# Attention in a two-layer RWKV-7/MLA decoder: the products with V of one query block written as one chain on TensorE, the later head first

## The chip, the cores and the metric

The kernel runs on one core of a Trainium2 chip. The metric is the device time of one launch in microseconds (us), lower is better. The kernel before was timed three times: median 1591.6 us, from 1591.0 to 1593.85 us.

## The reference, cut to what matters

Two decoder layers on 512 tokens of width 1024, batch 1, then a final RMSNorm. A layer is a mixer and a gated feed-forward part. The mixer has two branches: an RWKV-7 recurrence of 8 heads of 64, and MLA attention of 8 heads. Attention is causal and done in blocks of 128 queries:

```python
s = (jnp.einsum('bqhd,bkhd->bhqk', qn, k_nope)
     + jnp.einsum('bqhr,bkr->bhqk', qr, k_pe)).astype(jnp.float32) * scale
s = jnp.where(key_pos[None, :] <= q_pos[:, None], s, NEG_INF)
p = jax.nn.softmax(s, axis=-1).astype(v.dtype)
return jnp.einsum('bhqk,bkhd->bqhd', p, v)
...
merged = jax.nn.sigmoid(gate_a) * y_a + jax.nn.sigmoid(gate_b) * y_b
return merged @ w_out
```

The change concerns the last product of attention, P times V.

## The kernel before, in words

Everything is kept transposed: features on the 128 partitions, the 512 tokens along the free axis. Weights stream from memory in units of 128x1024 (`raw`); ScalarE and VectorE split each unit into a rounded part `whi` and a remainder `wlo`, activations are split likewise, and a weight block costs three matmuls in the one-pass type (lines 246 to 248, tile `acc`). These make up most of the kernel.

Attention stands in `mixer`, in `heads(p)` (line 907), called for p = 0 to 3. One call handles a pair of heads, hh = 0 and 1. It makes K and q of both heads and then goes through four query blocks b = 0 to 3, with b+1 key blocks each. For every (b, hh):

- the scores `sc` (line 929, one fp32 product of 128 x 128(b+1)),
- mask, scale and row minimum on VectorE (line 932), the exponential with its row sum on ScalarE (935), the reciprocal on VectorE (936), the scaling of P on ScalarE (937),
- the b+1 transposes of P on TensorE (line 940) into the one buffer `pt`, and a copy of `pt` into `PT` (line 942), by VectorE for b = 0 and 2, by ScalarE for b = 1 and 3. `PT` has three buffers.

Then come the 2(b+1) products with V (line 947): for every key block kb, first hh = 0, then hh = 1. The stationary side is 64 columns wide, so head 0 uses the left half of the array's columns and writes partitions 0 to 63 of `po`, head 1 the right half and partitions 64 to 127. `po` has one buffer, which is split into `oops` after the fourth block.

Around it stand the recurrence (lines 777 to 815) and its outputs: `chunk_out` (products of lines 833 and 841 into `xy`, copied by ScalarE, line 844), the group norm (lines 848 to 863, VectorE, ScalarE and a scaling on GpSimd), and `transposed` (line 869, transposes of `Z` into `xy`). Behind it are the output projections, lines 957 to 986.

The order in which the instructions stand on each engine is not the written one. A scheduler places them when the program is built: it takes instructions of different stages in turn, so that the first head pair's attention stands among the steps of the recurrence, and matmuls of lines 246 to 248 stand between attention's steps. Once placed, each engine works through its own list in that order, and an instruction waits for semaphores of other engines. Within `with tc.manual_schedule(engines={PE.engine})` TensorE's instructions keep the written order. In the kernel before, `heads` has no such block.

In the placed order of before, TensorE's list holds the products of line 947 of one block in pieces: the first product of head 0 by itself, then other work, then the rest.

Of the kernel before, what the change touches and what calls it, by code (L numbers as in the profile page):

```python
# [158 lines left out]
def build(ctx, tc, x, pos, wst, vecd, constd, out):  # L159
    nc = tc.nc  # L160
    V, A, G, PE = nc.vector, nc.scalar, nc.gpsimd, nc.tensor
# [83 lines left out]
    def mm3(ps, w, xx, first, last):  # L245
        PE.matmul(ps, w[0], xx[0], start=first, stop=False)  # L246
        PE.matmul(ps, w[0], xx[1], start=False, stop=False)  # L247
        PE.matmul(ps, w[1], xx[0], start=False, stop=last)  # L248
# [22 lines left out]
    def acc():  # L271
        return accp[-1].tile([128, 512], F32, name="acc", tag="acc")

    def split(pool, src, scale, tag, bufs=None):

        hi = pool.tile([128, 512], F32R, name="hi", tag=tag, bufs=bufs)
        lo = pool.tile([128, 512], F32R, name="lo", tag=tag, bufs=bufs)
        if scale is None:
            A.copy(hi, src)
            V.tensor_tensor(lo, src, hi.bitcast(F32), ALU.subtract)  # L280
        else:
            A.activation(hi, src, AF.Copy, scale=scale)  # L282
            V.scalar_tensor_tensor(lo, src, scale, hi.bitcast(F32), ALU.mult, ALU.subtract)
        return hi, lo
# [140 lines left out]
    def mixer(l, ops, nrm, wks):  # L425
        with ExitStack() as mx:
# [211 lines left out]
            def sc(name="sc"):  # L638
                return pb.tile([128, 512], F32, name=name, tag="sc", bufs=2)
# [7 lines left out]
            with pool(name=f"ti{l}", bufs=2) as ti, tc.manual_schedule(engines={PE.engine}):  # L647
# [94 lines left out]
                for b in range(2):  # L742
                    ps = sc()
                    for u in range(16 * b, 16 * b + 16):
                        for r0, c0 in half:
                            PE.matmul(ps[r0 + 32:r0 + 64, 32 * (u % 16):32 * (u % 16) + 32],
                                      AMu[r0:r0 + 32, u, c0 + 32:c0 + 64], T11[r0:r0 + 32, u, :],
                                      start=True, stop=True, tile_position=(r0, r0 + 32))
# [28 lines left out]
                for c in range(8):  # L777
# [22 lines left out]
                    if c < 7:  # L800
                        for p in range(4):
                            for hh in range(2):
                                hd = 2 * p + hh
# [13 lines left out]
            with pool(name=f"tb{l}", bufs=2) as tb:  # L817
                def MT(name, tag, bufs=3):
                    return tb.tile([128, 512], F32, name=name, tag=tag, bufs=bufs)
# [79 lines left out]
                Vt = tb.tile([128, 4, 512], F32, name="Vt", bufs=1)  # L899
# [7 lines left out]
                def heads(p):  # L907
                    psk = acc()
                    mm3(psk, [w[:, 128 * p:128 * p + 128] for w in lk], kvop, True, True)
                    qs, ks = [], []  # L910
                    for hh in range(2):
                        K = MT("K", "qk", 5)
                        A.copy(K[0:64, :], psk[64 * hh:64 * hh + 64, :])
                        G.tensor_copy(K[64:128, :], kp[64:128, :])
                        ks.append(K)
                    for hh in range(2):
                        psq = acc()
                        for j in range(2):
                            mm3(psq, W.get(), qops[j], j == 0, j == 1)
                        q = MT("q", "qk", 5)  # L920
                        V.tensor_tensor(q, psq, rq, ALU.mult)  # L921
                        qs.append(q)
                    po = pb.tile([128, 512], F32, name="po", tag="po")
                    for b in range(4):
                        n = 128 * (b + 1)
                        PTs = []
                        for hh in range(2):
                            sp = sc()
                            PE.matmul(sp[:, 0:n], qs[hh][:, 128 * b:128 * b + 128], ks[hh][:, 0:n], start=True, stop=True)  # L929
                            P = MT("P", "P")  # L930
                            mn = tb.tile([128, 4], F32, name="mn", bufs=4)
                            V.tensor_tensor_reduce(out=P[:, 0:n], in0=sp[:, 0:n],  # L932
                                                   in1=cst[:, C_CAUS + 512 - n:C_CAUS + 512], scale=-ATT_SCALE,
                                                   scalar=1e30, op0=ALU.add, op1=ALU.min, accum_out=mn[:, 0:1])
                            A.activation(P[:, 0:n], P[:, 0:n], AF.Exp, bias=mn[:, 0:1], scale=-1.0, accum_out=mn[:, 1:2])  # L935
                            V.reciprocal(mn[:, 2:3], mn[:, 1:2])  # L936
                            A.activation(P[:, 0:n], P[:, 0:n], AF.Copy, scale=mn[:, 2:3])  # L937
                            pt = pb.tile([128, 512], F32, name="pt", tag="pt")
                            for kb in range(b + 1):
                                PE.transpose(pt[:, 128 * kb:128 * kb + 128], P[:, 128 * kb:128 * kb + 128], ident)  # L940
                            PT = MT("PT", "PT")
                            (A.copy if b % 2 else V.tensor_copy)(PT[:, 0:n], pt[:, 0:n])  # L942
                            PTs.append(PT)
                        for kb in range(b + 1):
                            for hh in range(2):
                                hd = 2 * p + hh
                                PE.matmul(po[64 * hh:64 * hh + 64, 128 * b:128 * b + 128], Vt[:, kb, 64 * hd:64 * hd + 64],  # L947
                                          PTs[hh][:, 128 * kb:128 * kb + 128], start=kb == 0, stop=kb == b,
                                          tile_position=(0, 64 * hh))
                    oops.append(split(xp, po, None, "xb", 8))  # L950

                for f in (outputs, norms, lambda: heads(0), lambda: heads(1), transposed, lambda: heads(2), lambda: heads(3)):
                    f()
# [153 lines left out]
```

## Time and profile before

| | before |
|---|---|
| median of three runs | 1591.6 us (1591.0 to 1593.85) |
| the profiled execution, its own time | 1593.16 us |
| its span, from the first to the last instruction | 1591.4 us |
| mean granted TensorE clock | 0.997 |
| TensorE (PE) busy | 1562.6 us, 98% of the span |
| VectorE (DVE) / ScalarE (ACT) / GpSimd (POOL) busy | 58% / 42% / 12% |
| products with V, line 947 | 160 instructions, 320 records |

How to read it: "L947" is line 947 of the kernel before. An fp32 product leaves two records, one for each of its passes, so that "x2" in a row of line 947 or 929 is one product and "x6" three; transposes (line 940, 869) and the matmuls of lines 246 to 248 leave one. A matmul's duration includes the time in which it drains, which overlaps with the next one; what a step occupies on TensorE is the distance from its start to the start of what follows. Column "us" of a timeline is from the first start to the last end of a merged row, and brackets hold the engine's idle time before it and what ended it.

Attention lies in two places, one for each layer: from 264 to 353 us and from 1050 to 1139 us of the span.

### The profile page before, as it was taken

The page shows a single profiled execution, that of the slowest core. Times are in us where ns is not written, and L with a number is a line of the kernel's source. Part 1 is how long each engine was busy: PE and PEld are TensorE (multiplying, and loading weights), DVE is VectorE, ACT ScalarE, POOL GpSimd, SP SyncE. Part 2 cuts the span into 40 slices and gives each one's busy share as a digit, 9 for nine tenths or more (in the row PEclk, how much of TensorE's full clock was granted, in tenths as well). Part 3 has the DMA queues.
Part 4 walks back from the last instruction along what each step waited for, and adds up shares of the span by engine and source line. Part 5 has one row for each costly group of instructions (what it writes and reads, how often), then busy time and mean ns, then how long its engine had stood idle before and what let it go on. Part 6 is the DMA issues. An engine that isn't in the chain of part 4 may idle for free.

```text
span 1591.4 us, 22441 instructions
## 1 busy us (share of the span) xinstructions
PE 1562.6 (98%) x9052; PEld 1254.2 (79%) x9052; DVE 915.4 (58%) x1468; ACT 661.5 (42%) x996; POOL 184.7 (12%) x156
## 2 busy tenths in 40 slices
PE   8999999899999999999999999998999999999998
PEld 6878886668888888888878888775788888888887
DVE  6579786666555555533346668757564655554332
ACT  6445444563443333422244443446533434333222
POOL 1011102300311101100001111013002111010000
PEclk9999999999999999999999999999999999999999
DMA  5323322224423233233343233213253332332232
GB/s 192 125 100 132 121 81 67 88 74 147 123 96 99 93 97 102 93 108 120 110 146 106 94 106 120 74 48 101 86 162 103 97 102 93 95 104 93 93 104 82
DMA packets 57272, 166.08 MB, mean 104 GB/s; under 512 B 6352, under 2 KB 8528, under 8 KB 57168
## 3 DMA queue, kind: packets, MB, share of 16 engines
q1 hardware_dynamic: 57024, 164.48, 31.9%
q8 instruction: 71, 1.16, 0.3%
q14 instruction: 33, 0.27, 0.1%
q10 hardware_dynamic: 144, 0.16, 0.0%
HBM read 147.32 MB, written 17.30 MB: 103 GB/s over the span
## 4 chain that ended last, share of the span: by engine, by line
PE 91%; DVE 4%; issue 2%; ACT 1%; POOL 1%; DMA 0%; SPq 0%; POOLq 0%; DVEq 0%; ACTq 0%
PE acc L246 26%; PE acc L247 26%; PE acc L248 26%; PE sc L929 2%; PE po L947 2%; PE pt L940 1%; PE m L599 1%; PE xy L795 1%; DVE wlo L202 1%; PE m L607 1%; PE m L583 0%; PE xy L804 0%; PE m L524 0%; DVE X L661 0%; POOL mu L858 0%
## 5 line engine op out<-in xcount | busy, mean ns | idle before, releaser
L246 PE MATMUL acc<-hi,whi 128*128 128x512 f32 (+1 forms) x1910 | 752.4, 394 | 7.2 <-ACT hi L282 5.2
L248 PE MATMUL acc<-hi,wlo 128*128 128x512 f32 (+1 forms) x1910 | 742.6, 389 | 1.2 <-DVE wlo L202 1.2
L247 PE MATMUL acc<-lo,whi 128*128 128x512 f32 (+1 forms) x1910 | 742.8, 389 | 0.0
L201 ACT CAST whi<-raw 128x1024 fp32r<-128x1024 f32 (+2 forms) x249 | 253.5, 1019 | 547.2 <-PE acc L247 466.9
L246 PEld LDWEIGHTS acc<-hi,whi 128*128 128x128 f32 x1910 | 359.6, 188 | 82.5 <-ACT hi L282 5.2
L248 PEld LDWEIGHTS acc<-hi,wlo 128*128 128x128 f32 x1910 | 359.6, 188 | 76.1 <-DVE wlo L202 1.6
L247 PEld LDWEIGHTS acc<-lo,whi 128*128 128x128 f32 x1910 | 359.9, 188 | 72.4 <-issue 1.2
L202 DVE TENSOR_TENSOR wlo<-raw,whi 128x1024 fp32r<-128x1024 f32 (+2 forms) x249 | 309.5, 1244 | 175.9 <-ACT whi L201 175.5
L1027 POOL TENSOR_TENSOR c<-c,rstd 128x512 f32<-128x512 f32 x44 | 58.0, 1318 | 403.5 <-ACT c L1026 403.5
L1020 DVE TENSOR_TENSOR u<-acc,rstd 128x512 f32<-128x512 f32 x44 | 30.4, 692 | 104.7 <-PE acc L248 104.6
L1029 DVE TENSOR_TENSOR c<-c,acc 128x512 f32<-128x512 f32 x44 | 30.3, 688 | 86.4 <-POOL c L1027 86.4
L1026 ACT ACTIVATE c<-c 128x512 f32<-128x512 f32 x44 | 27.8, 632 | 81.6 <-DVE c L1025 81.6
L305 POOL TENSOR_TENSOR nv<-nv,cst 128x4 f32<-128x4 f32 (+1 forms) x10 | 10.0, 997 | 352.6 <-DVE nv L304 352.6
L341 POOL TENSOR_TENSOR nacc<-nacc,nsq 128x512 f32<-128x512 f32 x14 | 25.0, 1787 | 200.3 <-ACT nsq L340 200.3
L450 DVE TENSOR_TENSOR cur<-acc,rstd 128x512 f32<-128x512 f32 x28 | 19.1, 690 | 48.4 <-PE acc L248 39.3
L929 PE MATMUL sc<-K,q 128*128 128x128 f32 (+3 forms) x128 | 44.6, 446 | 1.1 <-DVE q L921 1.1
L935 ACT ACTIVATE P<-P,mn 128x128 f32<-128x128 f32 (+3 forms) x64 | 35.6, 556 | 17.2 <-issue 9.3
L932 DVE CUSTOM_DVE_ANT_0 P<-sc,cst 128x128 f32<-128x128 f32 (+3 forms) x64 | 30.7, 483 | 12.9 <-PE pt L940 10.4
L947 PE MATMUL po<-PT,Vt 128*64 128x128 f32 x320 | 37.5, 286 | 0.6 <-DVE PT L942 0.6
L937 ACT ACTIVATE P<-P,mn 128x128 f32<-128x128 f32 (+3 forms) x64 | 34.2, 557 | 6.6 <-DVE mn L936 6.6
L1023 ACT ACTIVATE c<-u,vec 128x512 f32<-128x512 f32 x44 | 35.7, 812 | 2.8 <-DVE u L1019 2.8
L947 PEld LDWEIGHTS po<-PT,Vt 128*64 128x64 f32 x320 | 22.3, 136 | 18.2 <-issue 7.3
(242 smaller groups left out, 1370.8 us busy)
## 6 DMA issues: line engine op xcount, KB each, us to landing
raw<-in_w SPq DMA_DIRECT2D x238, 512.0 KB, 3.4
gate_d<-gg SPq DMA_DIRECT2D x32, 256.0 KB, 2.1
AM<-gate_d SPq DMA_DIRECT2D x16, 256.0 KB, 5.9
gb<-gate_d SPq DMA_DIRECT2D x16, 256.0 KB, 3.6
h<-in_x SPq DMA_DIRECT2D x8, 256.0 KB, 4.6
rgate_d<-gt SPq DMA_DIRECT2D x8, 256.0 KB, 2.5
bl_d<-rk SPq DMA_DIRECT2D x8, 256.0 KB, 2.0
bl<-bl_d SPq DMA_DIRECT2D x8, 256.0 KB, 2.6
```

Source lines behind the costliest of these rows:

```text
L201: A.copy(hi, r)
L202: V.tensor_tensor(lo, r, hi.bitcast(F32), ALU.subtract)
L246: PE.matmul(ps, w[0], xx[0], start=first, stop=False)
L247: PE.matmul(ps, w[0], xx[1], start=False, stop=False)
L248: PE.matmul(ps, w[1], xx[0], start=False, stop=last)
L929: PE.matmul(sp[:, 0:n], qs[hh][:, 128 * b:128 * b + 128], ks[hh][:, 0:n], start=True, stop=True)
L932: V.tensor_tensor_reduce(out=P[:, 0:n], in0=sp[:, 0:n], in1=cst[:, C_CAUS + 512 - n:C_CAUS + 512], scale=-ATT_SCALE, scalar=1e30, op0=ALU. ...
L935: A.activation(P[:, 0:n], P[:, 0:n], AF.Exp, bias=mn[:, 0:1], scale=-1.0, accum_out=mn[:, 1:2])
L937: A.activation(P[:, 0:n], P[:, 0:n], AF.Copy, scale=mn[:, 2:3])
L947: PE.matmul(po[64 * hh:64 * hh + 64, 128 * b:128 * b + 128], Vt[:, kb, 64 * hd:64 * hd + 64], PTs[hh][:, 128 * kb:128 * kb + 128], start=k ...
L1023: A.activation(cc, u[:, 2:514], AF.Identity, bias=vc(l, "conv_b", i), scale=vc(l, "conv_w", 2 * FT + i))
L1027: G.tensor_tensor(cc, cc, rstd, ALU.mult)
```

## The change

The products with V of one block are put into a block with manual order for TensorE, and head 1 is taken before head 0 for every key block. Head 1 is the one whose P is transposed and copied last. The number of products, their operands, shapes and places in the array stay the same; the accumulation of each head runs over kb in the same order.

```diff
-                        for kb in range(b + 1):
-                            for hh in range(2):
-                                hd = 2 * p + hh
-                                PE.matmul(po[64 * hh:64 * hh + 64, 128 * b:128 * b + 128], Vt[:, kb, 64 * hd:64 * hd + 64],
-                                          PTs[hh][:, 128 * kb:128 * kb + 128], start=kb == 0, stop=kb == b,
-                                          tile_position=(0, 64 * hh))
+
+                        with tc.manual_schedule(engines={PE.engine}):
+                            for kb in range(b + 1):
+                                for hh in (1, 0):
+                                    hd = 2 * p + hh
+                                    PE.matmul(po[64 * hh:64 * hh + 64, 128 * b:128 * b + 128],
+                                              Vt[:, kb, 64 * hd:64 * hd + 64], PTs[hh][:, 128 * kb:128 * kb + 128],
+                                              start=kb == 0, stop=kb == b, tile_position=(0, 64 * hh))
```

The scheduler places the rest of the program around these chains anew, so that the lists of all engines change within the two attention stages. The product has line 949 in the changed kernel (later lines move by two). Below stands TensorE's list at two places of the first layer: `pt` are transposes of P, `sc` scores, `po` products with V, `xy<-cst,Z` transposes for the recurrence's output, `acc` the three-part matmuls.

The first place is on TensorE, blocks 0 and 1 of the second head pair. Before:

```order
L940 MATMUL pt<-cst,P 128x128
L929 MATMUL sc<-K,q 128x384
L947 MATMUL po<-PT,Vt 64x128
L940 MATMUL pt<-cst,P 128x128 x2
L869 MATMUL xy<-cst,Z 128x128
L929 MATMUL sc<-K,q 128x512 x2
L940 MATMUL pt<-cst,P 128x128 x2
L947 MATMUL po<-PT,Vt 64x128
L869 MATMUL xy<-cst,Z 128x128 x4
L947 MATMUL po<-PT,Vt 64x128 x3
```

The same place on TensorE now:

```order
L940 MATMUL pt<-cst,P 128x128
L929 MATMUL sc<-K,q 128x384
L949 MATMUL po<-PT,Vt 64x128 x2
L940 MATMUL pt<-cst,P 128x128 x2
L929 MATMUL sc<-K,q 128x512 x2
L940 MATMUL pt<-cst,P 128x128 x2
L869 MATMUL xy<-cst,Z 128x128
L949 MATMUL po<-PT,Vt 64x128 x4
```

Ahead of the upper rows stood, in the list of before, one more single product with V. The two products of block 0 and the four of block 1 now each stand together, and between the last transposes of block 1 and its products there is one transpose of line 869 instead of four and a product.

The second place is on TensorE just behind it, block 2 of the same pair, before:

```order
L940 MATMUL pt<-cst,P 128x128 x6
L947 MATMUL po<-PT,Vt 64x128 x6
L940 MATMUL pt<-cst,P 128x128 x4
L246 MATMUL acc<-hi,whi 128x512
L247 MATMUL acc<-lo,whi 128x512
L869 MATMUL xy<-cst,Z 128x128 x4
```

And now:

```order
L940 MATMUL pt<-cst,P 128x128 x3
L246 MATMUL acc<-hi,whi 128x512
L869 MATMUL xy<-cst,Z 128x128 x4
L247 MATMUL acc<-lo,whi 128x512
L248 MATMUL acc<-hi,wlo 128x512
L246 MATMUL acc<-hi,whi 128x512
L940 MATMUL pt<-cst,P 128x128 x3
L247 MATMUL acc<-lo,whi 128x512
L248 MATMUL acc<-hi,wlo 128x512
L929 MATMUL sc<-K,q 128x128
```

The transposes of the two heads, which stood in a row, now have other work between them and behind them; the six products of line 949 follow after one more row. In each layer the list of before holds the 80 products with V in 31 pieces, the list now in 17: one for each of 16 blocks, and one block (the first pair's fourth) in two pieces of six and two.

## Prediction

> **What bounds the kernel now.** First the page: how busy each engine is, and the chain that ended last.
>
> ```profile
> PE 1562.6 (98%) x9052; PEld 1254.2 (79%) x9052; DVE 915.4 (58%) x1468; ACT 661.5 (42%) x996; POOL 184.7 (12%) x156
> ...
> PE 91%; DVE 4%; issue 2%; ACT 1%; POOL 1%; DMA 0%; SPq 0%; POOLq 0%; DVEq 0%; ACTq 0%
> ```
>
> TensorE is busy for 98% of the span and makes 91% of the chain. Time is won where TensorE needs less for the same work, and lost where it begins to wait. The second view is TensorE's waits, of which attention's own are these (total, times, longest):
>
> ```profile
> PE pt L940 <- DVE mn L936: 1.5, 2, 0.7
> PE po L947 <- DVE PT L942: 0.6, 2, 0.3
> ```
>
> They are small. So the question is what the products with V occupy on TensorE. The third view, the groups by shape, gives their busy time, 37.5 us, but durations overlap:
>
> ```profile
> L947 PE MATMUL po<-PT,Vt 128*64 128x128 f32 x320 | 37.5, 286 | 0.6 <-DVE PT L942 0.6
> ```
>
> The timeline tells it by the distance between starts. A piece of one product, in block 0 of the second pair (first column the start, second the length):
>
> ```profile
> 303.16 0.43 PE L947 MATMUL po<-PT,Vt 128*64 128x128 f32 x2
> 303.52 0.33 PE L940 MATMUL pt<-cst,P 128*128 128x128 f32 x1
> 303.69 0.81 PE L929 MATMUL sc<-K,q 128*128 128x384 f32 x2
> 304.43 0.43 PE L947 MATMUL po<-PT,Vt 128*64 128x128 f32 x2
> ```
>
> One product takes 303.52 - 303.16 = 0.36 us; its partner stands at 304.43, a piece of its own. Pieces of three, five and seven products:
>
> ```profile
> 308.49 0.65 PE L947 MATMUL po<-PT,Vt 128*64 128x128 f32 x6
> 309.07 0.55 PE L940 MATMUL pt<-cst,P 128*128 128x128 f32 x3
> ...
> 311.53 0.87 PE L947 MATMUL po<-PT,Vt 128*64 128x128 f32 x10 [0.29 <-DVE PT L942]
> 312.33 0.66 PE L940 MATMUL pt<-cst,P 128*128 128x128 f32 x4
> ...
> 315.19 0.39 PE L247 MATMUL acc<-lo,whi 128*128 128x512 f32 x1
> 315.42 0.40 PE L248 MATMUL acc<-hi,wlo 128*128 128x512 f32 x1
> 315.75 1.09 PE L947 MATMUL po<-PT,Vt 128*64 128x128 f32 x14
> 316.76 0.71 PE L929 MATMUL sc<-K,q 128*128 128x128 f32 x4
> ```
>
> They take 0.58, 0.80 and 1.01 us: two products more cost 0.22 us. Head 1 and head 0 of neighbouring products run side by side, in one slot of 0.22 us; the rest of the 0.36, 0.14 us, is paid once for each piece. The trace has one block whose two products stand together:
>
> ```profile
> 340.60 0.44 PE L947 MATMUL po<-PT,Vt 128*64 128x128 f32 x4
> 340.97 0.44 PE L940 MATMUL pt<-cst,P 128*128 128x128 f32 x2
> ```
>
> Two products that both open their sum take 0.37 us, the price of one. A piece also slows its neighbours:
>
> ```profile
> 313.96 0.60 PE L940 MATMUL pt<-cst,P 128*128 128x128 f32 x4
> 314.49 0.43 PE L947 MATMUL po<-PT,Vt 128*64 128x128 f32 x2
> ...
> 331.60 0.60 PE L940 MATMUL pt<-cst,P 128*128 128x128 f32 x4
> 332.04 0.82 PE L929 MATMUL sc<-K,q 128*128 128x128 f32 x4
> ```
>
> Four transposes ahead of a piece take 0.53 us, ahead of scores 0.44: 0.09 us more. The `acc` row at 315.42 agrees (0.33 against 0.23 for the one at 315.19). Behind a piece a transpose takes 303.69 - 303.52 = 0.17 us, against 0.44/4 = 0.11: 0.06 us more. Together 0.15 us of neighbours for each piece.
>
> **The change, part by part.**
>
> *Head 1 first, all in a row: slots.* A block of b+1 key blocks has 2(b+1) products. Split after the first, they need one slot for the single one, b for pairs, and one for the last: b+2. In a row they need b+1. In each layer 15 of 16 blocks are split now (the row at 340.60 is the other): 30 slots of 0.22 us less, -6.6 us.
>
> *Fewer pieces.* By the lists, 31 pieces become 17 in each layer, 28 less in all: 28 x 0.14 = 3.9 us within, and 28 x 0.15 = 4.2 us on neighbours, if other engines do not make TensorE wait instead. Three pieces of each layer that stand beside the recurrence's products have cheaper neighbours, before and after alike. TensorE's work: -6.6 - 3.9 - 4.2 = -14.7 us. All of it lies on the path that sets the end, since TensorE is that path.
>
> *Waits that go.* At the second place shown of the list, six transposes and six products stand in a row with nothing between; there TensorE waits 0.29 us for `PT` (311.53) and 0.7 us for the reciprocal, in each layer: 0.6 + 1.5 = 2.1 us by the rows of waits. The new list has `acc` and transposes of line 869 at both spots, more than 1 us. I count -2.1 us.
>
> *Waits that come.* The chain now starts with the head whose copy ends last, and TensorE's whole list is queued behind it. At the first place shown, block 1:
>
> ```profile
> 307.23 0.38 PE L940 MATMUL pt<-cst,P 128*128 128x128 f32 x2
> ```
> ```profile
> 307.64 0.37 ACT L942 COPY PT<-pt 128x256 f32<-128x256 f32 x1 [0.42 <-PE pt L940]
> ...
> 314.60 0.59 ACT L942 COPY PT<-pt 128x512 f32<-128x512 f32 x1 [0.96 <-PE pt L940]
> ```
>
> The copy ends at 308.01, 0.78 us after the first of the two transposes began. The new list covers this with two transposes and one of line 869: 0.11 + 0.11 + 0.20 = 0.42. That is a wait of 0.36, in two layers 0.7 us. Two more spots lose cover, where attention stands between the recurrence's outputs:
>
> ```profile
> 293.08 0.69 PE L833 MATMUL xy<-St,AR 64*64 64x64 f32 x32 [0.35 <-ACT Z L844]
> ...
> 300.55 0.33 PE L869 MATMUL xy<-cst,Z 128*128 128x128 f32 x1 [1.16 <-POOL Z L863]
> ```
>
> Ahead of each the new list has one `acc` matmul less, 0.23 us by the row at 315.19; both waits grow by as much, 0.46 a layer, 0.9 in two. In the other blocks at least a score product (0.74 us at 303.69) or several `acc` matmuls stand between the last transpose and the chain. Named waits: +1.6 us.
>
> *The softmax chain behind it.* With less on TensorE between scores and transposes, ScalarE and VectorE have less time for P. In the stage of pairs 1 to 3, from the first scores to the last copy:
>
> ```profile
> 298.20:352.90 54.70, 52.37 (x294) 33.72 (x296) 36.00 (x112) 38.79 (x97) 7.25 (x7) 1.00 0.21 63
> ```
>
> The columns are length, then busy time of PE, PEld, DVE, ACT and POOL: ScalarE is busy for 38.79 of 54.70 us, and TensorE waits for 54.70 - 52.37 = 2.33. I bound the tightening by 0 (ScalarE keeps up) and by the whole saving of this stage (below), and take half of those 2.33 us once more in each layer: +2.4 us. I lean to the low end because most of ScalarE's idle time there is waiting for TensorE itself:
>
> ```profile
> L942 ACT COPY PT<-pt 128x256 f32<-128x256 f32 (+1 forms) x12 | 5.7, 476 | 5.4 <-PE pt L940 5.3
> L279 ACT CAST hi<-po 128x512 fp32r<-128x512 f32 x2 | 1.2, 587 | 2.3 <-PE po L947 2.3
> ```
>
> No instruction of DMA is added or taken away, and the weights' queue keeps its order; what moves on VectorE, ScalarE and GpSimd has cover as long as TensorE sets the pace.
>
> Sum: -14.7 - 2.1 + 1.6 + 2.4 = -12.8 us. The profiled execution took 1593.2 us, 1.8 of it around its span, and would take 1580.4. The median of the runs lies 1.6 us below it: 1578.8 us.
>
> One rule speaks against the largest term. The Trainium skill, TensorE: Matmul & The Clock Gate, Part 3 ("What overlaps and what doesn't"), says that a weight load overlaps with matmuls in flight only when their row groups differ; the two heads differ in columns alone, so by it they would not share a slot. This trace disagrees: three products take 0.58 us, not 0.36 + 2 x 0.22 = 0.80. By that rule the sum would be -6.2 us.
>
> **The rivals.**
>
> *Softmax sets the pace.* The saving of pairs 1 to 3 is 11 slots and 11 pieces a layer, 11 x (0.22 + 0.14 + 0.15) = 5.6 us. If ScalarE and VectorE give nothing, all of it returns as waits: 11.2 us instead of the 2.4, so -12.8 - 2.4 + 11.2 = -4.0 and 1587.6 us. For it: ScalarE, 71% busy there, would have to reach 38.79 / (54.70 - 5.6) = 79%, and its list runs in order. Against it: the 7.6 us of waits in the two rows above shrink by themselves when TensorE comes sooner.
>
> *Each chain waits for its copy (slower).* If nothing covered the copy of head 1, each of 32 chains would wait from its last transpose's start to the copy's end: 0.78 - 0.11 = 0.67 us in block 1, 315.19 - 313.96 - 0.33 = 0.90 in block 3, mean 0.79, or 25.3 us. Then -14.7 - 2.1 + 25.3 = +8.5, 1600.1 us. It decides from 16.8/32 = 0.53 us of uncovered wait per chain. The lists speak against it: in the second place shown, as in most, `acc` matmuls stand there.
>
> *No shared slots.* Pairs of heads run one after the other in the chain: the -6.6 falls away, -6.2 is left, 1585.4 us. The row at 340.60 and the pieces of three, five and seven speak against it; the rule cited above would have it so.
>
> **How the numbers follow.** My forecast of 1578.8 us has 80%, softmax 10%, the slower chain 3%, no shared slots 3%; 4% is for less than the range's low end. That end is without the softmax term and with dearer neighbours:
>
> ```profile
> 321.60 0.91 PE L929 MATMUL sc<-K,q 128*128 128x384 f32 x2
> 322.44 0.43 PE L947 MATMUL po<-PT,Vt 128*64 128x128 f32 x2
> ```
>
> These scores, behind a piece, take 0.84 us, those at 303.69 behind a transpose 0.74. With 0.05 more per piece, 28 x 0.05 = 1.4: -14.7 - 1.4 - 2.1 + 1.6 = -16.6, 1575.0 us. The high end is 1586.0, which takes in the case without shared slots and most of the way to softmax's 1587.6. A measurement of this kernel can tell about 0.2%, 3.2 us, from no change; softmax's 1587.6 lies beside that bound and is counted half as faster, half as within. Faster: 0.80 + 0.05 + 0.03 + 0.04 = 0.92; within 0.2%: 0.05; slower: 0.03.
>
> **What would show it.** In the changed profile, 34 pieces of line 949; a block of one, two, three and four key blocks at 0.36, 0.58, 0.80 and 1.01 us from start to start; busy time of these products well below 37.5 us; a wait of `po` for ScalarE's `PT` of about 0.4 us in block 1 of the second pair; the reciprocal's wait gone. It would be wrong if the waits of TensorE for `PT`, `P` or `mn` together grew by more than 6 us, if the opening pair of a chain did not share a slot, or if the stages behind attention, all TensorE, did not begin sooner by what was saved.

## Result, and the profile after

The changed kernel takes 1577.55 us (median of five runs, 1577.11 to 1578.71); the kernel before took 1593.12 us beside it (five runs, 1591.0 to 1593.85). The ratio is 0.9907, 95% interval 0.9896 to 0.9918: faster by 0.9%. The profiled execution took 1577.86 us, with a span of 1575.7 us against 1591.4.

The page of the changed kernel, busy time and the chain:

```profile
PE 1547.2 (98%) x9052; PEld 1248.5 (79%) x9052; DVE 916.1 (58%) x1468; ACT 659.9 (42%) x996; POOL 183.7 (12%) x156
...
PE 91%; DVE 5%; ACT 2%; issue 2%; POOL 0%; DMA 0%; SPq 0%; DVEq 0%; POOLq 0%; ACTq 0%
```

TensorE runs the same 9052 records in 1547.2 us instead of 1562.6, 15.4 less. Span minus busy time is 28.5 us where it was 28.8. So all that was won is TensorE's work, and its idle time as a whole stayed.

TensorE's timeline in the second head pair has one block of each size (first column the start, second the length):

```profile
301.50 0.44 PE L949 MATMUL po<-PT,Vt 128*64 128x128 f32 x4
301.87 0.44 PE L940 MATMUL pt<-cst,P 128*128 128x128 f32 x2
...
304.15 0.27 PE L869 MATMUL xy<-cst,Z 128*128 128x128 f32 x1
304.77 0.66 PE L949 MATMUL po<-PT,Vt 128*64 128x128 f32 x8 [0.35 <-ACT PT L942]
305.36 0.55 PE L940 MATMUL pt<-cst,P 128*128 128x128 f32 x3
...
308.47 0.88 PE L949 MATMUL po<-PT,Vt 128*64 128x128 f32 x12
309.28 0.66 PE L940 MATMUL pt<-cst,P 128*128 128x128 f32 x4
...
312.32 1.09 PE L949 MATMUL po<-PT,Vt 128*64 128x128 f32 x16
313.35 0.66 PE L869 MATMUL xy<-cst,Z 128*128 128x128 f32 x4
```

Two, four, six and eight products stand in one row each and take 0.37, 0.59, 0.81 and 1.03 us from start to start: one slot of 0.22 us for each key block, and 0.15 us for the piece. Counted over the whole timeline, with idle time taken off:

| products in a piece | before: pieces, us of one | after: pieces, us of one |
|---|---|---|
| 1 | 36, 0.363 | none |
| 2 | 2, 0.370 | 10, 0.370 |
| 3 / 4 | 8, 0.582 / none | none / 8, 0.589 |
| 5 / 6 | 6, 0.800 / 4, 0.83 to 1.23 | none / 10, 0.807 |
| 7 / 8 | 6, 1.018 / none | none / 6, 1.025 |
| all | 62 pieces, 33.3 us | 34 pieces, 22.5 us |

(Medians. In two of the pieces of six of before, the first product stands apart from the other five by the wait for `PT` at 311.53, which is taken off.) The products with V take 10.8 us less. The other 4.6 of the 15.4 us lie on what stands beside them.

TensorE's waits in the whole run (total, times, longest), the rows that changed or were forecast to:

```profile
PE xy L869 <- POOL Z L863: 2.3, 2, 1.2
PE xy L833 <- ACT Z L844: 2.1, 4, 0.6
PE sc L929 <- DVE q L921: 1.5, 2, 0.8
...
PE po L949 <- ACT PT L942: 0.7, 2, 0.4
```

The waits for the reciprocal (1.5) and for VectorE's `PT` (0.6) are gone. New is the wait of 0.7 us for ScalarE's `PT`, the 0.35 us at 304.77 in each layer. The one of line 833 rose from 1.3 to 2.1, the one for `q` from 1.1 to 1.5, and the one for GpSimd's `Z` stayed at 2.3.

### The profile page after: what moved, and what is told of

The parts are those of the page before. It is cut to its first block, busy times and chain, and to the rows that moved or that the text cites. A ratio compares the mean times of both kernels' runs of the same rounds, so it can differ in the third digit from the quotient of the medians.

```text
span 1575.7 us, 22425 instructions
## 1 busy us (share of the span) xinstructions
PE 1547.2 (98%) x9052; PEld 1248.5 (79%) x9052; DVE 916.1 (58%) x1468; ACT 659.9 (42%) x996; POOL 183.7 (12%) x156
## 3 DMA queue, kind: packets, MB, share of 16 engines
q8 instruction: 71, 1.16, 0.3%
## 4 chain that ended last, share of the span: by engine, by line
PE 91%; DVE 5%; ACT 2%; issue 2%; POOL 0%; DMA 0%; SPq 0%; DVEq 0%; POOLq 0%; ACTq 0%
PE acc L246 26%; PE acc L247 26%; PE acc L248 26%; PE sc L929 2%; PE pt L940 1%; PE po L949 1%; PE m L599 1%; PE xy L795 1%; DVE wlo L202 1%; PE m L607 1%; PE m L583 1%; PE xy L804 0%; PE m L524 0%; DVE X L661 0%; DVE tm L659 0%
## 5 line engine op out<-in xcount | busy, mean ns | idle before, releaser
L1027 DVE SCALAR_TENSOR_TENSOR c<-u,vec,c 128x512 f32<-128x512 f32 x44 | 33.1, 752 | 1.5
L1026 DVE SCALAR_TENSOR_TENSOR c<-u,vec,c 128x512 f32<-128x512 f32 x44 | 32.8, 746 | 1.8 <-ACT c L1025 1.8
```

What stands on the lines that cost most here:

```text
L1026: V.scalar_tensor_tensor(cc, u[:, 1:513], vc(l, "conv_w", FT + i), cc, ALU.mult, ALU.add)
L1027: V.scalar_tensor_tensor(cc, u[:, 0:512], vc(l, "conv_w", i), cc, ALU.mult, ALU.add)
```

## Experiments

The theory: products with V cost TensorE by pieces (about 0.29 us each, 0.14 within and 0.15 on neighbours) and by slots (0.22 us each, two heads sharing one), and taking head 1 first removes both. The rivals: the block with manual order does it; slots aren't shared, or only by direct neighbours; the pieces' price is only what is seen within them; what is won comes from waits.

**One half of the change at a time.** First the manual block with the old order of heads:

```diff
-                                for hh in (1, 0):
+                                for hh in (0, 1):
```

> The manual block is kept, but head 0 is taken first. The lists of all engines come out word for word as in the kernel before, with 31 pieces of products with V in each layer. Theory (pieces and slots): the time of before, within 0.2%, ratio to before 1.000. Rival (the manual block is what helps): about 0.990, as the changed kernel.

Measured: 1592.42 us, before 1592.36 beside it, ratio 1.0001 (0.9992 to 1.001). Then the new order of heads without the block:

```diff
-                        with tc.manual_schedule(engines={PE.engine}):
-                            for kb in range(b + 1):
-                                for hh in (1, 0):
...
+                        for kb in range(b + 1):
+                            for hh in (1, 0):
```

> Head 1 first, without the manual block. The lists come out word for word as in the changed kernel, 17 pieces in each layer. Theory (pieces and slots; the order of the heads alone makes them): the time of the changed kernel, ratio to before 0.990 to 0.991. Rival (the manual block is what helps): 1.000.

Measured: 1578.75 us (1575.22 to 1580.27), ratio 0.9904 (0.989 to 0.9917), as the whole change. The lists of instructions of the first kernel are, word for word, those of before, those of the second the ones of the changed kernel. So the order of the heads is the whole change. The block with manual order keeps its products in their order but does not keep them together: with head 0 first, the scheduler places the product that has its `PT` and then other work, block or not. With head 1 first, nothing can be placed until the later `PT` is there, and then everything can.

**Both heads, but not in turn.** All products of head 1, then all of head 0:

```diff
-                            for kb in range(b + 1):
-                                for hh in (1, 0):
+                            for hh in (1, 0):
+                                for kb in range(b + 1):
```

> The changed kernel, but within a block all products of head 1 stand ahead of all of head 0, so that only the last of head 1 and the first of head 0 can share a slot. Pieces stay whole, 17 in each layer (one of them cut seven to one in place of six to two). Slots of a block of b+1 key blocks grow from b+1 to 2b+1, 6 more for each head pair, 48 in all. Theory (a slot is 0.22 us): 48 x 0.22 = 10.6 us over the changed kernel, some 1588 us, ratio to before 0.997. Rival (the piece alone has a price, products cost the same in any order): as the changed kernel, ratio 0.990.

Measured: 1583.1 us (1581.29 to 1586.47), ratio 0.9942 (0.9928 to 0.9955). Its timeline in the second pair:

```profile
305.99 0.67 PE L949 MATMUL po<-PT,Vt 128*64 128x128 f32 x8 [0.35 <-ACT PT L942]
306.58 0.55 PE L940 MATMUL pt<-cst,P 128*128 128x128 f32 x3
...
309.69 1.15 PE L949 MATMUL po<-PT,Vt 128*64 128x128 f32 x12
310.77 0.66 PE L940 MATMUL pt<-cst,P 128*128 128x128 f32 x4
...
313.82 1.58 PE L949 MATMUL po<-PT,Vt 128*64 128x128 f32 x16
315.33 0.66 PE L869 MATMUL xy<-cst,Z 128*128 128x128 f32 x4
```

Four products take 0.59 us, as in turn; six take 1.08 instead of 0.81, eight 1.51 instead of 1.03. All pieces together take 28.5 us, 6.0 more than in turn, and the kernel 5.6 us more than the changed one at its first median (4.4 more than the kernel without the block, measured beside it). Its profile has 13.7 us at a clock of 0.50 up to the last matmul, so the sum over the pieces is the better measure of the two. Both are about half of the 10.6 us expected: the expectation, with one shared slot left in each block, missed. That the slot is shared is shown: what separates the two heads in the list makes the piece dearer. But sharing isn't limited to direct neighbours. Two, three and four products of each head take 2, 4 and 6 slots (0.15 + 0.22 x 2, 4, 6 = 0.59, 1.03, 1.47), where no sharing would take 4, 6 and 8: two slots are saved each time (the eight products take 0.04 us more than this sum), as if a product of the other half could run beside one up to two places ahead.

**The price of a piece.** One transpose of the identity in blocks 1 and 2, 16 in all, ahead of the chain or inside it:

```diff
                         with tc.manual_schedule(engines={PE.engine}):
+                            if b in (1, 2):
+                                PE.transpose(pt[:, 384:512], ident, ident)
                             for kb in range(b + 1):
```
```diff
                             for kb in range(b + 1):
+                                if kb == 1 and b < 3:
+                                    PE.transpose(pt[:, 384:512], ident, ident)
                                 for hh in (1, 0):
```

> The changed kernel with one more transpose (the identity into an unused part of pt, its result is not read) just ahead of the chain of blocks 1 and 2: 16 transposes of a full-width mode in all, no chain is cut. Both theories: 16 x 0.11 = 1.8 us over the changed kernel. It is the yardstick for the kernel with the same transpose inside the chain.

> The same transpose, now inside the chain of blocks 1 and 2, between the first pair of products and the rest: 16 chains are cut in two, pairs and slots stay. Theory (a piece costs 0.14 us within and 0.15 us on its neighbours): 16 x 0.29 = 4.6 us over the kernel with the transpose ahead of the chain. Rival 1 (only the 0.14 us within): 2.2 us. Rival 2 (cutting costs nothing, the gain was slots and waits): no difference.

Measured: ahead 1578.34 us, ratio 0.9909 (0.9895 to 0.9922); inside 1582.11 us, ratio 0.9934 (0.992 to 0.9947), 3.8 us more at the median. The first layer's attention stage, from the first scores to the last product with V (columns: length, then busy time of PE, PEld, DVE, ACT, POOL, the granted clock, the DMA's share and GB/s), ahead and inside:

```profile
263.20:344.72 81.52, 77.29 (x794) 54.67 (x792) 56.55 (x168) 56.12 (x136) 15.07 (x15) 1.00 0.20 64
```
```profile
263.70:347.01 83.31, 79.11 (x794) 54.54 (x792) 56.78 (x168) 56.08 (x136) 15.05 (x15) 1.00 0.20 63
```

The stage has the same 794 records and eight pieces more, at full clock in both, and is 83.31 - 81.52 = 1.79 us longer: 0.22 us for each piece. The products themselves take 24.9 instead of 22.5 us, 0.15 for each of the 16 new pieces. So the price within is as predicted, and on neighbours 0.07 is left in the mean. The mean hides two prices. Place by place, from the start of the row ahead of the chain to the start of the row behind it, with idle time taken off, the cut costs 0.15 us at eight of the 16 places and 0.30 at the other eight. It costs 0.30 where an `acc` or a score product stands ahead of the chain without a wait, as in block 2 of the second pair, ahead and inside:

```profile
308.62 0.48 PE L246 MATMUL acc<-hi,lk 128*128 128x512 f32 x1
308.93 0.27 PE L947 MATMUL pt<-cst 128*128 128x128 f32 x1
309.14 0.88 PE L951 MATMUL po<-PT,Vt 128*64 128x128 f32 x12
309.94 0.66 PE L940 MATMUL pt<-cst,P 128*128 128x128 f32 x4
```
```profile
309.56 0.48 PE L246 MATMUL acc<-hi,lk 128*128 128x512 f32 x1
309.97 0.44 PE L951 MATMUL po<-PT,Vt 128*64 128x128 f32 x4
310.34 0.33 PE L948 MATMUL pt<-cst 128*128 128x128 f32 x1
310.60 0.66 PE L951 MATMUL po<-PT,Vt 128*64 128x128 f32 x8
311.19 0.66 PE L940 MATMUL pt<-cst,P 128*128 128x128 f32 x4
```

From the first to the last of these rows it is 1.32 us ahead and 1.63 inside. It costs 0.15 where a wait or the recurrence's narrow products stand ahead of the chain: there the transpose takes 0.26 us in both kernels, and nothing is added beside the piece. So neither expectation fits as a whole (16 x 0.29 = 4.6 us, 16 x 0.14 = 2.2, and 3.6 to 3.8 were measured), but 0.29 fits where nothing else slows the neighbours already.

The kernel with the transposes ahead takes only 0.3 to 0.8 us more than the changed one, where 1.8 were expected. Its stages have full clock throughout, which the last pair of runs below comes back to. In the first layer, where both kernels have full clock, its stage is 2.30 us longer than the changed kernel's, with five `acc` matmuls (1.15 us) and these eight transposes more: 0.14 us for each.

**Fewer pieces still.** The products of blocks 0 and 1 in one chain, eight pieces less. `PT` gets two buffers for each of three sizes, and for their room a scratch tile of the group norm becomes 16 wide instead of 24:

```diff
-                            PT = MT("PT", "PT")
+                            PT = tb.tile([128, 512 if b > 1 else n], F32, name="PT", tag=f"PT{min(b, 2)}", bufs=2)
...
+                        todo.append((b, PTs))
+                        if b:
+                            with tc.manual_schedule(engines={PE.engine}):
+                                for bb, pts in reversed(todo):
+                                    for kb in range(bb + 1):
+                                        for hh in (1, 0):
...
+                            todo = []
```

> The changed kernel, but blocks 0 and 1 of a head pair put their products into one chain, block 1 first; PT has two buffers for each size in place of three large ones, and the group norm's small tile is narrower. 13 pieces in each layer in place of 17, slots unchanged. Theory (a piece is 0.14 us within and 0.15 us on its neighbours): 8 x 0.29 = 2.3 us under the changed kernel, ratio to before 0.989. Rival (the piece has no price of its own, all of the gain was slots and waits): no difference to the changed kernel, or slower where buffers run short.

Measured: 1579.03 us (1577.72 to 1582.53), ratio 0.9917 (0.9903 to 0.9931). The waits of this kernel:

```profile
PE xy L869 <- POOL Z L863: 4.9, 4, 2.1
```

The pieces fall to 26 and the products to 21.4 us, 1.1 less or 0.14 for each piece, as priced. But with the lists placed anew TensorE waits 4.9 us instead of 2.3 for GpSimd's `Z`, and nothing is won. The price within a piece shows again; what the scheduler makes of the rest can't be told from it.

**Can the other waits be had as well?** `transposed`, whose transposes wait for GpSimd, one head pair later; then instead the first pair ahead of the recurrence's outputs; then each of these with the chains of blocks 0 and 1 joined:

```diff
-                for f in (outputs, norms, lambda: heads(0), lambda: heads(1), transposed, lambda: heads(2), lambda: heads(3)):
+                for f in (outputs, norms, lambda: heads(0), lambda: heads(1), lambda: heads(2), transposed, lambda: heads(3)):
```
```diff
-                for f in (outputs, norms, lambda: heads(0), lambda: heads(1), transposed, lambda: heads(2), lambda: heads(3)):
+                for f in (lambda: heads(0), outputs, norms, lambda: heads(1), transposed, lambda: heads(2), lambda: heads(3)):
```

> The changed kernel, with the transposes for the recurrence's output called one head pair later, behind the third pair. The third transpose of line 869, where TensorE waited 1.16 us in each layer for GpSimd's scaling, stands seven rows further down; chains, pieces and slots stay. If waits set by other engines' chains are what is left in this stage, the 2.3 us for GpSimd and part of the 1.2 for ScalarE go, and no 3.4 us window of half clock follows them: 2 to 4 us under the changed kernel, ratio to before 0.988 to 0.989. Rival (the waits only move, since ScalarE's and VectorE's list sets them): no difference, 0.990 to 0.991.

> The changed kernel, with the first head pair called ahead of the recurrence's outputs. Scores and chains then stand between the products of lines 833 and 841, where TensorE waited 2.1 us for ScalarE, and line 869 has more ahead of it; 16 pieces in each layer in place of 17. If those waits are worth their rows: up to 2.1 + 2.3 + 1.2 = 5.6 us less and 2 x 0.29 for the pieces, so 3 to 6 us under the changed kernel, ratio to before 0.987 to 0.989. Rival (softmax sets the pace once the waits are gone): no difference, 0.990 to 0.991.

> Both: the first head pair ahead of the recurrence's outputs, and the products of blocks 0 and 1 in one chain: 12 pieces in each layer. If the price of a piece holds and the waits that ate it in the kernel with joined blocks were those of line 869: 8 x 0.29 = 2.3 us under the kernel with the first pair ahead alone. Rival (joining costs as much in waits as it saves in pieces, wherever those transposes stand): no difference to that kernel.

> Both: the transposes for the recurrence's output one pair later, and the products of blocks 0 and 1 in one chain, 13 pieces in each layer. If the waits of line 869 were what hid the price of the piece in the kernel with joined blocks: 2.3 us under the kernel with the later transposes alone. Rival (joining costs as much in waits as it saves): no difference to that kernel.

| kernel | us, median | ratio to before |
|---|---|---|
| `transposed` later | 1574.86 (1574.46 to 1576.79) | 0.9896 (0.9882 to 0.9909) |
| first pair ahead | 1585.13 (1583.14 to 1587.21) | 0.9959 (0.9947 to 0.9972) |
| first pair ahead, joined chains | 1583.94 (1581.4 to 1585.78) | 0.995 (0.9937 to 0.9962) |
| `transposed` later, joined chains | 1576.76 (1573.79 to 1578.28) | 0.9899 (0.9884 to 0.9914) |

With `transposed` later the wait for GpSimd is gone, and others stand in its place. The waits of the first layer's stage:

```profile
PE pt L940 <- ACT P L937: 1.3, 2, 1.1
PE xy L833 <- ACT Z L844: 1.0, 2, 0.6
PE sc L929 <- DVE q L921: 1.0, 1, 1.0
```

TensorE idles 4.2 us in this stage, with `transposed` earlier 4.3, before the change 4.3: the softmax and the recurrence's output need their time, and moving one wait brings out another. Its ratio of 0.9896 lies between the two expectations, and the interval overlaps that of the changed kernel. Taking the first pair ahead is the miss: GpSimd's `Z` then costs TensorE 6.4 us in five waits, 4.1 more than in the changed kernel, and up to the last matmul its profile has 13.7 us at a clock of 0.50 where the changed kernel's has 3.4. The joined chains bring nothing that shows to either: the intervals overlap those of the same order without them.

**A cost that comes and goes.** The changed kernel's two attention stages differ, though their lists and idle times are alike. The windows of the changed kernel's profile (after the five busy times stand the granted clock, the DMA's share and GB/s), both stages, and three neighbouring stretches of 3.41 us in the second:

```profile
263.40:342.62 79.22, 74.93 (x781) 52.54 (x779) 57.05 (x168) 55.54 (x136) 15.06 (x15) 1.00 0.20 61
1040.70:1121.55 80.85, 76.56 (x781) 53.62 (x779) 57.14 (x168) 55.53 (x136) 15.06 (x15) 0.98 0.20 60
```
```profile
1072.38:1075.79 3.41, 1.51 (x7) 1.07 (x8) 3.36 (x13) 2.88 (x10) 2.68 (x2) 1.00 0.03 7
1075.79:1079.20 3.41, 3.41 (x9) 2.27 (x9) 2.09 (x8) 1.19 (x5) 1.16 (x1) 0.50 0.47 151
1079.20:1082.61 3.41, 3.41 (x16) 1.67 (x15) 1.48 (x7) 2.01 (x8) 1.89 (x3) 1.00 0.01 2
```

The second stage is 1.63 us longer. In it TensorE idled 3.41 - 1.51 = 1.90 us of one window, the waits for `q` and for GpSimd's `Z` having fallen into it together, and in the next its clock was 0.50. To test that idle time does this, six transposes of the identity fill it in each layer, between the second and third transpose of the first pair; the changed kernel ran beside it once more, as it is:

```diff
                     for i in range(4):
+                        if p == 0 and i == 2:
+                            for _ in range(6):
+                                PE.transpose(ps[:, 256:384], ident, ident)
                         PE.transpose(ps[:, 128 * i:128 * i + 128], Z[:, i, 0, 128 * p:128 * p + 128], ident)
```

> The changed kernel with six more transposes of the identity on TensorE in each layer, between the second and the third transpose of line 869 of the first pair, where TensorE waits 0.77 us for q and 1.16 us for Z within 3 us. They go into a part of ps that is written later by the scores; what they make is not read. Theory (the clock of TensorE is halved for 3.4 us behind a window of 3.4 us in which TensorE idles for more than about 1.6 us): with 6 x 0.11 = 0.66 us of that idle time filled, no window of the rows has half clock in either layer's attention stage, both stages are about 79 us from the first scores to the last product, and the time is up to 1.6 us below that of the changed kernel beside it, 1576 to 1577 us, ratio about 0.990. Rival (the half clock comes by itself, not from idle time): it appears in attention as in the changed kernel, and the time is the changed kernel's or up to 1.3 us (12 transposes) above it.

> The changed kernel once more, as it is, beside the one with filled idle time. Both theories: ratio about 0.9907. By the theory of idle time a run has a window of half clock in one or both attention stages where the 0.77 and the 1.16 us fall into one window of 3.4 us, and none where they fall into two, about 1.6 us between the cases, so that single runs spread over some 1575 to 1580 us.

Measured: filled, 1575.92 us (four runs, 1575.36 to 1577.2), ratio 0.99 (0.9886 to 0.9915); as it is, 1578.05 us (four runs: 1575.65, 1576.76, 1579.33, 1579.64), ratio 0.9908 (0.9891 to 0.9924). The stages, filled:

```profile
263.11:342.56 79.45, 75.80 (x787) 53.20 (x785) 57.04 (x168) 55.49 (x136) 15.04 (x15) 1.00 0.19 61
...
1040.41:1119.84 79.43, 75.78 (x787) 53.18 (x785) 57.09 (x168) 55.49 (x136) 15.04 (x15) 1.00 0.19 61
```

And in the second run of the changed kernel:

```profile
264.43:345.23 80.80, 76.51 (x781) 53.64 (x779) 57.10 (x168) 55.52 (x136) 15.04 (x15) 0.98 0.19 60
1042.47:1123.31 80.84, 76.57 (x781) 53.62 (x779) 57.06 (x168) 55.52 (x136) 15.04 (x15) 0.98 0.18 60
```

Filled, no window has half clock in either stage, both take 79.4 us, and the runs lie within 1.8 us. The same changed kernel has such a window in one stage in its first profile and in both in its second, 80.8 us each. For the attention stages the profiles bear the theory out. The runs do so too by the granted clock of each: of the 14 runs with the changed kernel's lists, three have 0.998 or more and take 1575.2 to 1575.7 us, five have 0.997 (1576.8 to 1577.9), four 0.996 (1578.7 to 1579.3) and two 0.995 (1579.6 to 1580.3). But idle time isn't the only occasion. In the kernel with the manual block and head 0 first, TensorE is busy through the whole window ahead of one with half clock:

```profile
200.87:204.28 3.41, 3.41 (x52) 2.99 (x51) 3.24 (x9) 1.47 (x2) 0.00 (x0) 1.00 0.33 130
204.28:207.69 3.41, 3.41 (x9) 2.67 (x10) 2.97 (x7) 1.98 (x4) 1.16 (x1) 0.50 0.43 125
```

What brings it there is open. The two medians differ by 2.1 us, more than the 1.6 expected, but the intervals of the ratios overlap, so a gain over the changed kernel is not shown by the times alone. The same goes for the kernel with `transposed` later, the fastest median here; its profile too has both stages at full clock.

## Why the prediction was right, point by point

*Slots and pieces within, -6.6 - 3.9 = -10.5 us.* Measured -10.8, with 62 pieces become 34 and the four lengths to within 0.02 us of the forecast. That head order and not the manual block brings it was not predicted.

*Neighbours, -4.2 us.* What is left of TensorE's busy time is -4.6. Over the whole timeline a transpose of P just ahead of a piece takes 0.20 us and one just behind it 0.17, against 0.11 among its like; a score product takes 0.09 us more ahead of a piece and 0.10 more behind it, an `acc` matmul 0.10 more on either side. Summed over the neighbours of all pieces that is 9.9 us before (0.16 for each piece) and 4.7 after (0.14), 5.2 less, so it accounts for the 4.6; some 0.6 us came back elsewhere on TensorE. (The recurrence's narrow products are counted as unslowed, and an `acc` that starts while an fp32 row still runs is counted together with it.) So the 0.15 read from single rows holds; the 0.07 of the experiment is a mean over places of which half had slowed neighbours already. Both profiles have one window of 3.41 us at half clock before the last matmul (before at 22.4 us, after at 1075.8), so that isn't it.

*Waits that go, -2.1.* As forecast.

*Waits that come, +1.6.* Measured +0.7 for `PT` as forecast, +0.8 for line 833 (forecast 0.46), nothing for line 869 (0.46), and +0.4 for `q`, which was not forecast: 1.9 in all.

*The softmax allowance, +2.4.* It didn't come, and this is the term of the sum that was mis-sized. TensorE idles 4.29 us in the stage where it idled 4.28. The reason given for the low end was the right one. ScalarE's groups of pairs 1 to 3 in the changed kernel (last columns: idle time ahead and what ended it):

```profile
L942 ACT COPY PT<-pt 128x256 f32<-128x256 f32 (+1 forms) x12 | 5.7, 473 | 1.4 <-PE pt L940 1.2
...
L279 ACT CAST hi<-po 128x512 fp32r<-128x512 f32 x2 | 1.1, 566 | 0.0
```

These were 5.4 and 2.3 us of ScalarE's waiting and are 1.4 and 0. ScalarE gave up its own waits for TensorE, and TensorE paid nothing for it, though ScalarE is now busy for more than the 79% that the rival asked:

```profile
295.82:341.36 45.54, 43.82 (x281) 29.66 (x281) 34.93 (x111) 37.61 (x96) 6.70 (x7) 1.00 0.19 59
```

37.61 of 45.54 us is 83%, while TensorE idles 1.72 us there.

*The sum.* -12.8 was forecast, and the profiled span fell by 15.7: of the 2.9 between them 2.4 are the allowance, 0.4 neighbours and 0.3 products; the named waits took 0.3 back. The median of 1577.55 us lies 1.25 below the 1578.8 given; from the 1593.12 measured for before beside it, -12.8 would have been 1580.3. That the median came so close is in part luck: the kernel before measured 1.5 us more than in its first three runs, and that hid half of the error. The gain itself is 15.6 us here and 13.6 and 14.0 in two later sets (1578.75 beside 1592.36, 1578.05 beside 1592.02), with the windows of half clock in it.

*The rivals.* Softmax as the pace: no, by the idle time above. Each chain waiting for its copy: one spot a layer, 0.35 us each. No shared slots: eight products take 1.03 us, where eight slots of 0.22 alone would be 1.76. The rule cited for it, of the Trainium skill, TensorE: Matmul & The Clock Gate, Part 3 ("What overlaps and what doesn't"), speaks of weight loads; that products in two column halves could then not share a slot was the prediction's own step, and it doesn't hold here. One part of the order was left out of the forecast: where the waits of 0.77 and 1.16 us stand. They can now fall into one window of the clock, which costs 1.6 us a layer in some executions and none in others.

## What to carry to other kernels

Where two short chains of products share an engine's array, look at the list for pieces: here it paid to put the operand that is ready last first, since the scheduler split the chain behind the first product whose inputs came early. Price a piece by the distance from start to start, and its neighbours over the whole list; an experiment that makes more pieces gives a mean over its places, which need not be those of the change. And before an allowance is made for the engines behind the bound, count how much of their idle time is waiting for that bound itself: it shrinks first.

## What the runs showed of the hardware

Idle time of TensorE that doesn't fill a window was followed by half clock in the attention stages: 1.90 us of 3.41 were enough in the second layer, and the 2.10 us of one wait in the kernel with joined chains were too:

```profile
298.68:302.09 3.41, 1.31 (x7) 0.83 (x8) 3.12 (x10) 2.34 (x8) 3.19 (x3) 1.00 0.13 28
302.09:305.50 3.41, 3.41 (x10) 2.60 (x9) 0.59 (x3) 0.63 (x3) 2.47 (x2) 0.50 0.32 129
```

The wait for `Z` stands in the upper window, and the lower one has a clock of 0.50. In the first layer of the changed kernel the window held less:

```profile
294.14:297.55 3.41, 1.80 (x8) 1.07 (x8) 3.36 (x14) 2.88 (x7) 2.64 (x3) 1.00 0.03 10
297.55:300.96 3.41, 2.82 (x13) 2.11 (x14) 2.94 (x8) 1.82 (x8) 1.38 (x2) 1.00 0.18 55
```

1.61 us of idle time, and the next window kept full clock. The kernel with the heads not in turn had just as much in its second layer, and there the next window had half clock:

```profile
1076.09:1079.50 3.41, 1.80 (x9) 1.07 (x8) 3.04 (x10) 2.00 (x6) 2.66 (x3) 1.00 0.03 10
1079.51:1082.92 3.41, 2.26 (x7) 1.67 (x7) 2.83 (x6) 1.67 (x6) 1.13 (x2) 0.50 0.09 18
```

So in these stages the border lies near 1.6 us; closer it was not measured. It isn't a rule for the whole run: the window at 204.28 us above had half clock without idle time ahead of it, and ahead of the changed kernel's first matmul, which starts at 5.19 us, 3.41 us without any matmul (0.60 to 4.01) were followed by a granted clock of 1.00. The windows stand on a grid of their own: in the two profiles of the changed kernel the same waits fell once into two windows and three times into one. The Trainium skill, TensorE: Matmul & The Clock Gate, Part 1 ("What's actually happening"), has the free-running window of 3413 ns and half clock after an idle window; the length agrees with the 3.41 us seen here, while a window idle for about half of it was enough.

Products in the two column halves of the array share a slot of 0.22 us, and not only direct neighbours do: with two, three and four of each head not in turn, 2, 4 and 6 slots were taken. A piece of these half-width products costs 0.15 us beyond its slots where it stands between full-width ones, and 0.15 to 0.20 more on the two rows beside it (0.09 to 0.10 ahead, 0.06 to 0.10 behind).
